# Two diffusion layers on one core: the high halves of the mixers' weight blocks move from ScalarE to GpSimd

## Chip, cores and metric

The kernel runs on one core of a Trainium2 chip, in one launch. The metric is device time in microseconds (us), the median of several runs; lower is better.

## What is computed

The reference is a backbone of two layers over 256 latent tokens and 256 context tokens, 1024 features wide. Each layer is a half-step feed-forward block, a mixer with three groups of channels, and a second half-step feed-forward block. All of it is in 32-bit floats. Cut to what matters here:

```python
for l in range(2):
    x     = x     + 0.5 * mx[2] * swiglu(ada_norm(x, ...),     w_ffn_in[l, 0], w_ffn_out[l, 0])
    h_ctx = h_ctx + 0.5 * mc[2] * swiglu(ada_norm(h_ctx, ...), w_ffn_in[l, 0], w_ffn_out[l, 0])
    # mixer: one projection hx @ w_in, hc @ w_in, split into
    #   q, k, v      -> head norms, rotary, attention
    #   u, g         -> conv of width 4, gates, scans both ways, times gelu(g)
    #   b, c, s      -> b * conv3(c * s)
    # each group RMS-normalised, concatenated, times w_out
    out_x, out_c = mixer(ada_norm(x, ...), ada_norm(h_ctx, ...), p, cos, sin, not last)
    x = x + mx[5] * out_x
    x = x + 0.5 * mx[8] * swiglu(ada_norm(x, ...), w_ffn_in[l, 1], w_ffn_out[l, 1])
    # layer 0 does the same for h_ctx
return rms_norm(x, final_norm_g)
```

## The kernel before

Activations lie with features on the 128 partitions and tokens along the free dimension: columns 0 to 255 are context, 256 to 511 latent. The weights are packed on the host as one list of blocks of 128x1024 floats (`PLAN`), in the order in which the program uses them. TensorE multiplies in the fast rounded format fp32r, so each 32-bit operand is split into a rounded high half and a low half that holds the remainder. `mm3` (lines 326 to 328) makes one product of three matmuls: high by high, high by low, low by high. Names in the profile follow from that: `hh`, `hl` are the halves of the normed input, `hi`, `lo` those of a weight block, `gh`, `gl` those of the feed-forward's inner activation, `mh`, `ml` those of the mixer's merged output.

A weight block goes through three stations. SyncE's queue loads it into one of seven `raw` buffers (L147). Then `split` (lines 131 to 133) makes its halves, in one of five pairs of `hi` and `lo` buffers:

```python
def split(hi, lo, src):
    act(hi, src, AF.Copy)                      # L132, ScalarE
    tt(lo, src, f(hi), OP.subtract)            # L133, VectorE
```

Then TensorE uses the halves. With five pairs, the high half of a block can be written only when TensorE is done with the block five before it. `get` (a step's call for its next block) runs `advance`, which splits two blocks ahead of the one asked for.

Of the 310 blocks of 128x1024 that are split in this way, the two mixers use 24 each: four first blocks of the input projection (`mi`), the k and v columns (`kv`, two blocks), the q columns (`q`, four), six more `mi` blocks for the short convolution (`sc` steps), and eight blocks of the output projection (`mo`). The feed-forward blocks (`wi`, `wo`) use the rest.

A mixer is written as small steps (`kv`, `qp`, `ka`, `qb`, `sm`, `tr`, ...), and the tables `ORDER[0]` and `ORDER[1]` give the sequence of the steps by hand. The framework then makes one queue for each engine out of the program, by what each instruction waits for and by its own estimate of when that is ready; each engine takes its queue strictly in order. So when an instruction goes to another engine, a few of its neighbours change places too. In a mixer, VectorE does the remainder `lo`, the rotary products of q and k (`qo`, `q`), the split of their rows (`kr`, `qr`, by way of L132 and L133 too), the taps of the convolutions (`uc`, `sc`), the scans (`tl`) and the row maxima of the scores (`nb`). ScalarE does the exponentials (`P`), the tanh and the logarithms of the gates (`th`, `a`), copies out of PSUM (`kT`, `qT`, `PT`) and the high halves. TensorE transposes the rows of k and q (L697, L735) before it makes scores (L870). GpSimd does nothing but clear five small tiles at the start.

Of the kernel before, what the change touches and what calls it, by code (L numbers as in the profile page):

```python
# [13 lines left out]
OP = mybir.AluOpType  # L14
# [92 lines left out]
def hybrid_block_kernel(ctx: ExitStack, tc, wpk, xin, pp, cc, cct, qkg, rope, lruw, ident, out):  # L107
    nc = tc.nc
# [9 lines left out]
    stt, tt, ts = vec.scalar_tensor_tensor, vec.tensor_tensor, vec.tensor_scalar  # L118

    def f(ap):  # L120
        return ap.bitcast(F32)
# [5 lines left out]
    def T(dt=F32, name="t"):  # L127
        t = tp.tile([128, 512], dt, tag="t", name=name)
        return t

    def split(hi, lo, src):
        act(hi, src, AF.Copy)  # L132
        tt(lo, src, f(hi), OP.subtract)  # L133
# [9 lines left out]
    def dma_to(i):  # L143
        while nxt_dma[0] <= min(i, len(PLAN) - 1):
            j = nxt_dma[0]
            r = raw4("raw")
            nc.sync.dma_start(r, wpk[j])  # L147
            raws[j] = r
            nxt_dma[0] += 1
# [95 lines left out]
    def mod_unit(l, m, t, raw):  # L245
        for v in range(2):
            junk = tp.tile([128, 1024], BF16, tag="t", name="junk")
            stt(junk, raw, 1.0, CB[v], op0=OP.mult, op1=OP.mult, accum_out=mod_col(l, m, t, v))  # L248
        if t == 7:
            mod_finish(l, m, slice(0, 8))  # L250
# [3 lines left out]
    def mod_products(m, b, i, raw):  # L254


        if m == 1 and i == 0:
            mp[b] = bank()
        c = (1 - m) * 256
        for j in range(4):  # L260
            nc.tensor.matmul(mp[b][32 * j:32 * j + 32, c:c + 256], ccT[:, 4 * i + j, :],
                             raw[:, j * 256:(j + 1) * 256], start=i == 0, stop=i == 1)
        if m == 0 and i == 1:
            row = T(name="modrow")
            act(row, mp[b], AF.Copy)
            pt = bank()
            for t in range(4):
                nc.tensor.transpose(pt[:, t * 128:(t + 1) * 128], row[:, t * 128:(t + 1) * 128], idf)
            sums = const.tile([128, 4, 2], F32, tag="psum4", name="psum4", bufs=2)
            vec.tensor_reduce(sums, pt.rearrange("p (t j c) -> p t c j", t=4, j=4)[:, :, 0:2], axis=AX.X, op=OP.add)  # L270
            for v in (1, 0):
                mod_finish(0, v, slice(2 * b, 2 * b + 2), sums[:, 2 - 2 * v:4 - 2 * v])
# [16 lines left out]
    def advance(i):  # L289

        while nxt[0] <= min(i, len(PLAN) - 1):
            j = nxt[0]
            u = PLAN[j]
            r = raws.pop(j)
            if u[0] == "m":
                mod_unit(u[1], u[2], u[3], r)
            elif u[0] == "p":
                mod_products(*u[2:], r)
            elif WPOS[4] <= j < WPOS[HEAD0]:
                parts = [(T(F32R, "w0h"), T(F32R, "w0l")) for _ in range(2)]  # L300
                for p, (hi, lo) in enumerate(parts):
                    split(hi, lo, r[:, p * 512:(p + 1) * 512])
                ready[j] = [tuple(x[:, i * 128:(i + 1) * 128] for x in p) for p in parts for i in range(4)]
            else:
                hi = wp.tile([128, 1024], F32R, tag="hi", name="hi")
                lo = wp.tile([128, 1024], F32R, tag="lo", name="lo")
                split(hi, lo, r)
                if u[0] in ("kv", "q"):
                    ready[j] = (hi, lo)
                else:  # L310
                    ready[j] = [(hi[:, i * 128:(i + 1) * 128], lo[:, i * 128:(i + 1) * 128]) for i in range(8)]
            nxt[0] += 1
            dma_to(j + RAWB)
# [3 lines left out]
    def get(key, ahead=2):  # L317
        n = nw[0]
        assert PLAN[WPOS[n]] == key, (PLAN[WPOS[n]], key)
        advance(WPOS[min(n + ahead, len(WPOS) - 1)])  # L320
        nw[0] += 1
        return ready.pop(WPOS[n])
# [706 lines left out]
    def first_head(h, units):  # L1029
# [10 lines left out]
        def block(b):  # L1040
            advance(PLAN.index(("p", 0, 0, b, 1)))
            for k in (2 * b, 2 * b + 1):
                h.make(k, FULL)
# [147 lines left out]
```

## Time and profile before

| what | value |
|---|---|
| three runs | 1664.17, 1664.75, 1665.06 us; median 1664.75 |
| the profiled execution | 1665.47 us, of which the profile's span is 1663.7 us |
| TensorE (PE) busy | 1620.4 us, 97% of the span, granted clock 0.994 on average |
| VectorE (DVE) busy | 1124.9 us, 68% |
| ScalarE (ACT) busy | 673.9 us, 41% |
| GpSimd (POOL) busy | 0.5 us, five instructions |

The profile shows one execution. A busy share is an average over stages, so it says little about a stage in which another engine sets the pace. The mixers run from about 390 to 605 us (layer 0) and from about 1315 to 1470 us (layer 1) of the span; the feed-forward blocks and the modulation products fill the rest. A row of the timeline gives start, duration, engine, line and operation, and in brackets how long the engine sat idle before it and what ended that.

### The profile page before, as it was taken

How to read it: one execution, taken by the hardware profiler on the slowest of the kernel's cores; microseconds unless marked ns; L12 is line 12 of the kernel's file. 1: busy time of each engine (PE TensorE's matmuls, PEld its weight loads, DVE VectorE, ACT ScalarE, POOL GpSimd, SP SyncE). 2: the span in 40 equal slices, each digit the busy share in tenths (PEclk: the TensorE clock that was granted, in tenths of full speed). 3: DMA queues.
4: the chain of work that ended last, by engine and by line, in shares of the span. 5: the costliest groups of instructions: out<-in, count | busy, mean ns of one | idle time of the engine just before them, and what ended most of it. 6: DMA issues, size and time to landing. Idle time of an engine off the chain costs nothing.

```text
span 1663.7 us, 21498 instructions
## 1 busy us (share of the span) xinstructions
PE 1620.4 (97%) x8396; PEld 1357.9 (82%) x8396; DVE 1124.9 (68%) x1894; ACT 673.9 (41%) x1073; POOL 0.5 (0%) x5
## 2 busy tenths in 40 slices
PE   7999999999999999999999999999999998999997
PEld 3888888889886898888888898888888887788886
DVE  4667757677697676784667665573555678866666
ACT  4432122323877453322223243222223378655453
POOL 0000000000000000000000000000000000000000
PEclk9999999999999999999999999999999999999999
DMA  8555645553321125564555524453444433245551
GB/s 332 179 184 177 219 136 180 176 176 127 114 78 37 41 72 183 188 207 135 176 176 167 165 95 146 165 177 115 152 141 150 152 102 102 83 146 189 184 185 38
DMA packets 68502, 247.25 MB, mean 149 GB/s; under 512 B 7728, under 2 KB 8240, under 8 KB 68400
## 3 DMA queue, kind: packets, MB, share of 16 engines
q1 hardware_dynamic: 67392, 244.87, 44.2%
q8 instruction: 66, 1.08, 0.3%
q10 hardware_dynamic: 1008, 1.00, 0.2%
q14 instruction: 36, 0.29, 0.1%
HBM read 244.80 MB, written 1.05 MB: 148 GB/s over the span
## 4 chain that ended last, share of the span: by engine, by line
PE 92%; DVE 4%; ACT 3%; DMA 1%; issue 0%; DVEq 0%; ACTq 0%; SPq 0%
PE ps L326 25%; PE ps L327 25%; PE ps L328 25%; PE ps L333 7%; PE ps L334 3%; DVE lo L133 1%; PE ps L902 1%; PE ps L801 1%; PE ps L870 1%; ACT hi L132 1%; PE ps L884 1%; PE ps L386 1%; ACT P L874 1%; PE ps L1021 0%; DVE ht L426 0%
## 5 line engine op out<-in xcount | busy, mean ns | idle before, releaser
L132 ACT ACTIVATE hi<-raw 128x1024 fp32r<-128x1024 f32 x310 | 327.7, 1060 | 789.3 <-PE ps L327 576.4
L133 DVE TENSOR_TENSOR lo<-raw,hi 128x1024 fp32r<-128x1024 f32 x310 | 378.6, 1223 | 196.4 <-ACT hi L132 194.8
L326 PE MATMUL ps<-hh,hi 128*128 128x512 f32 (+1 forms) x1344 | 487.1, 367 | 8.6 <-ACT hh L427 8.0
L328 PE MATMUL ps<-hh,lo 128*128 128x512 f32 (+1 forms) x1344 | 489.6, 365 | 0.8 <-DVE lo L133 0.7
L327 PE MATMUL ps<-hl,hi 128*128 128x512 f32 (+1 forms) x1312 | 480.8, 368 | 3.7 <-DVE hl L430 3.6
L248 DVE SCALAR_TENSOR_TENSOR junk<-raw,cb 128x1024 bf16<-128x1024 f32 x256 | 302.0, 1219 | 13.2 <-DMA raw<-in_wpk_dram 13.2
L326 PEld LDWEIGHTS ps<-hh,hi 128*128 128x128 f32 x1344 | 252.3, 190 | 51.6 <-ACT hh L427 9.7
L328 PEld LDWEIGHTS ps<-hh,lo 128*128 128x128 f32 x1344 | 255.3, 190 | 42.5 <-DVE lo L133 2.3
L327 PEld LDWEIGHTS ps<-hl,hi 128*128 128x128 f32 x1312 | 248.0, 189 | 45.7 <-DVE hl L430 5.3
L326 PE MATMUL ps<-gh,hi 128*128 128x512 f32 (+1 forms) x594 | 217.6, 366 | 0.0
L327 PE MATMUL ps<-gl,hi 128*128 128x512 f32 (+1 forms) x594 | 217.1, 365 | 0.0
L328 PE MATMUL ps<-gh,lo 128*128 128x512 f32 (+1 forms) x594 | 217.1, 365 | 0.0
L524 DVE TENSOR_TENSOR gf<-gf,ps 128x512 f32<-128x512 f32 (+1 forms) x68 | 46.2, 679 | 175.7 <-PE ps L328 174.5
L327 PEld LDWEIGHTS ps<-gl,hi 128*128 128x128 f32 x594 | 112.0, 189 | 18.2
L326 PEld LDWEIGHTS ps<-gh,hi 128*128 128x128 f32 x594 | 112.1, 189 | 18.2
L328 PEld LDWEIGHTS ps<-gh,lo 128*128 128x128 f32 x594 | 112.0, 189 | 18.0
L444 DVE SCALAR_TENSOR_TENSOR xT<-ps,modT,xT 128x256 f32<-128x256 f32 x176 | 79.9, 479 | 65.8 <-PE ps L328 55.5
L333 PE MATMUL ps<-hh,hi 128*128 128x512 f32 x320 | 113.2, 399 | 0.0
L334 PE MATMUL ps<-hh,lo 128*128 128x256 f32 x320 | 89.9, 281 | 0.0
L333 PEld LDWEIGHTS ps<-hh,hi 128*128 128x128 f32 x320 | 60.1, 188 | 14.9
L333 PE MATMUL ps<-gh,hi 128*128 128x512 f32 x176 | 62.2, 398 | 0.1
L334 PEld LDWEIGHTS ps<-hh,lo 128*128 128x128 f32 x320 | 60.5, 189 | 0.0
(203 smaller groups left out, 1601.2 us busy)
## 6 DMA issues: line engine op xcount, KB each, us to landing
raw<-in_wpk_dram SPq DMA_DIRECT2D x456, 512.0 KB, 3.3
xT<-in_xin_dram SPq DMA_DIRECT2D x4, 512.0 KB, 5.4
cb<-in_cc_dram SPq DMA_DIRECT2D x4, 512.0 KB, 3.7
lw<-in_lruw_dram SPq DMA_DIRECT2D x2, 512.0 KB, 4.1
out_dram<-y SPq DMA_DIRECT2D x2, 256.0 KB, 2.7
out_dram<-y ACTq DMA_DIRECT2D x2, 256.0 KB, 2.8
pps<-in_pp_dram ACTq DMA_DIRECT2D x1, 138.0 KB, 6.5
qkb<-in_qkg_dram ACTq DMA_DIRECT2D x1, 128.0 KB, 3.2
```

Of the source, the lines that this page charges most:

```text
L132: act(hi, src, AF.Copy)
L133: tt(lo, src, f(hi), OP.subtract)
L248: stt(junk, raw, 1.0, CB[v], op0=OP.mult, op1=OP.mult, accum_out=mod_col(l, m, t, v))
L326: nc.tensor.matmul(ps, wh, xh, start=first, stop=False)
L327: nc.tensor.matmul(ps, wh, xl, start=False, stop=False)
L328: nc.tensor.matmul(ps, wl, xh, start=False, stop=last)
L333: nc.tensor.matmul(ps, wh, xx, start=first, stop=False)
L334: nc.tensor.matmul(ps[:, 0:256], wl, xx[:, 0:256], start=False, stop=last)
L386: nc.tensor.matmul(st[:, a:b], ones[n], x[:, a:b], start=i == 0, stop=i == len(parts) - 1)
L444: stt(xT[:, k, a:b], ps[:, a - left:b - left], mod_col(l, m, k, v), xT[:, k, a:b], op0=OP.mult, op1=OP.add)
L524: tt(gf[:, a:b], gf[:, a:b], pu[:, a:b], OP.mult)
L801: nc.tensor.matmul(ps, lw[:, c * 128:(c + 1) * 128], uc, start=True, stop=True)
```

## The change

In `advance`, blocks of the kinds `mi`, `kv`, `q` and `mo` get their high half from GpSimd instead of ScalarE; VectorE makes the low half as before. Feed-forward blocks are left with `split`.

```diff
                 hi = wp.tile([128, 1024], F32R, tag="hi", name="hi")
                 lo = wp.tile([128, 1024], F32R, tag="lo", name="lo")
-                split(hi, lo, r)
+                if u[0] in ("mi", "kv", "q", "mo"):
+
+                    nc.gpsimd.tensor_copy(hi, r)
+                    tt(lo, r, f(hi), OP.subtract)
+                else:
+                    split(hi, lo, r)
```

Lines behind the edit move down by five, and the remainder of a mixer block is L310 instead of L133. GpSimd's queue is, behind the clearing of `ccT` at the start, the 48 copies (`CAST hi<-raw 128x1024`, L309) with nothing between them. The queues of the other engines change in some places, by the framework's own choice; three of them are shown, all on VectorE.

The first place is in the mixer of layer 1, where the gates end: `ge` is the gelu, `a` the gate product, `th` and `tl` its input and its scan. Before:

```order
L792 SCALAR_TENSOR_TENSOR ge<-ge,g 128x256
L813 SCALAR_TENSOR_TENSOR a_11104<-a_11104,tl 128x512
L133 TENSOR_TENSOR lo<-raw,hi 128x1024
L828 TENSOR_TENSOR th<-th,a_11104 128x512
L832 SCALAR_TENSOR_TENSOR tl<-th 128x256
L834 SCALAR_TENSOR_TENSOR tl<-th,tl 128x256
```

Now:

```order
L797 SCALAR_TENSOR_TENSOR ge<-ge,g 128x256
L310 TENSOR_TENSOR lo<-raw,hi 128x1024
L818 SCALAR_TENSOR_TENSOR a_11104<-a_11104,tl 128x512
L833 TENSOR_TENSOR th<-th,a_11104 128x512
L837 SCALAR_TENSOR_TENSOR tl<-th 128x256
L839 SCALAR_TENSOR_TENSOR tl<-th,tl 128x256
```

A `lo` (that of the last block of q columns) has moved ahead of the gate product.

The second place is some rows later in the same mixer, where the first rows of q get their rotary products (`q`, `qo`, with the small head norm `hr`) and are split into `qr`. Before:

```order
L666 TENSOR_TENSOR q_11372<-ps,rope_615 128x8x32
L650 TENSOR_SCALAR hr<-hr 128x16
L667 TENSOR_TENSOR qo<-qo,q_11372 128x512
L651 SCALAR_TENSOR_TENSOR hr<-hr 128x16
L668 TENSOR_TENSOR qo<-qo,hr 128x512
L133 TENSOR_TENSOR lo<-raw,hi 128x1024
L133 TENSOR_TENSOR qr<-qo,qr 128x4x64 x2
```

Now:

```order
L671 TENSOR_TENSOR q_11372<-ps,rope_615 128x8x32
L655 TENSOR_SCALAR hr<-hr 128x16
L672 TENSOR_TENSOR qo<-qo,q_11372 128x512
L656 SCALAR_TENSOR_TENSOR hr<-hr 128x16
L310 TENSOR_TENSOR lo<-raw,hi 128x1024
L673 TENSOR_TENSOR qo<-qo,hr 128x512
L133 TENSOR_TENSOR qr<-qo,qr 128x4x64 x2
```

The `lo` has moved ahead of the last rotary product; it stands ahead of `qr` in both.

The third place is in the mixer of layer 0, from the first to the second rows of q; `uc` is the recurrent group's output. Before:

```order
L133 TENSOR_TENSOR qr<-qo,qr 128x4x64 x2
L832 SCALAR_TENSOR_TENSOR tl<-th 128x256
L828 TENSOR_TENSOR th<-th,a_3503 128x512
L659 TENSOR_TENSOR qo<-ps,qkb 128x512
L834 SCALAR_TENSOR_TENSOR tl<-th,tl 128x256
L668 TENSOR_TENSOR qo<-qo,hr 128x512
L133 TENSOR_TENSOR lo<-raw,hi 128x1024
L133 TENSOR_TENSOR qr<-qo,qr 128x4x64 x2
L842 TENSOR_TENSOR uc<-tl 128x512
L832 SCALAR_TENSOR_TENSOR tl<-th 128x256
L843 SCALAR_TENSOR_TENSOR uc<-uc,ge 128x512
```

Now:

```order
L839 SCALAR_TENSOR_TENSOR tl<-th,tl 128x256
L673 TENSOR_TENSOR qo<-qo,hr 128x512
L847 TENSOR_TENSOR uc<-tl 128x512
L133 TENSOR_TENSOR qr<-qo,qr 128x4x64 x2
L310 TENSOR_TENSOR lo<-raw,hi 128x1024
L664 TENSOR_TENSOR qo<-ps,qkb 128x512
L848 SCALAR_TENSOR_TENSOR uc<-uc,ge 128x512
L673 TENSOR_TENSOR qo<-qo,hr 128x512
L833 TENSOR_TENSOR th<-th,a_3503 128x512
L133 TENSOR_TENSOR qr<-qo,qr 128x4x64 x2
```

Two operations on `uc` of 128x512 have moved ahead of the second `qr`; the `lo` that stood ahead of it still does.

## Rows read from the trace of the kernel before

**Rows 1.** The page, part 1: busy time, share, instructions; part 4: the chain.
```profile
PE 1620.4 (97%) x8396; PEld 1357.9 (82%) x8396; DVE 1124.9 (68%) x1894; ACT 673.9 (41%) x1073; POOL 0.5 (0%) x5
PE 92%; DVE 4%; ACT 3%; DMA 1%; issue 0%; DVEq 0%; ACTq 0%; SPq 0%
```

**Rows 2.** Busy time by stage: first mixer, feed-forward blocks, second mixer; then PE, PEld, DVE, ACT.
```profile
390.00:605.00 215.00, 209.49 (x1280) 176.48 (x1280) 161.35 (x310) 141.28 (x281) 0.00 (x0) 1.00 0.21 70
605.00:1315.00 710.00, 709.48 (x3373) 598.14 (x3373) 450.73 (x680) 208.14 (x266) 0.00 (x0) 1.00 0.48 157
1315.00:1470.00 155.00, 139.80 (x933) 119.89 (x933) 124.59 (x237) 108.12 (x208) 0.00 (x0) 0.97 0.29 96
```

**Rows 3.** The page, part 5: the two halves of a weight block.
```profile
L132 ACT ACTIVATE hi<-raw 128x1024 fp32r<-128x1024 f32 x310 | 327.7, 1060 | 789.3 <-PE ps L327 576.4
L133 DVE TENSOR_TENSOR lo<-raw,hi 128x1024 fp32r<-128x1024 f32 x310 | 378.6, 1223 | 196.4 <-ACT hi L132 194.8
```

**Rows 4.** Groups of GpSimd's instructions, whole span.
```profile
L169 POOL MEMSET ccT<- 128x256 f32 x1 | 0.3, 312 | 0.3 <-POOLq L1179 0.3
L1179 POOL MEMSET const-float32-0.0<- 128x1 f32 x1 | 0.1, 99 | 0.2 <-issue 0.2
```

**Rows 5.** Groups of VectorE's instructions by form, 1363.6 to 1384.1 us.
```profile
L133 DVE TENSOR_TENSOR lo<-raw,hi 128x1024 fp32r<-128x1024 f32 x7 | 8.5, 1219 | 0.7 <-ACT hi L132 0.5
L644 DVE TENSOR_REDUCE hr<-sq 128x8 f32<-128x512 f32 x3 | 1.9, 675 | 0.0
...
L666 DVE TENSOR_TENSOR q<-ps,rope 128x256 f32<-128x256 f32 x2 | 0.8, 418 | 0.0
```

**Rows 6.** Timeline of TensorE, second mixer: two waits for VectorE, one for ScalarE.
```profile
1377.66 1.22 PE L697 MATMUL ps<-idr,kr 128*128 128x128 f32 x12 [0.91 <-DVE kr L133]
1384.62 0.68 PE L735 MATMUL ps<-idr,qr 128*128 128x128 f32 x3 [2.51 <-DVE qr L133]
1414.23 1.09 PE L884 MATMUL ps<-idf,P 128*128 128x128 f32 x8 [1.89 <-ACT PT L889]
```

**Rows 7.** Busy time in one stretch of 5 us behind the second wait; 0.66 is the clock.
```profile
1385.00:1390.00 5.00, 5.00 (x19) 3.57 (x20) 3.89 (x9) 2.27 (x4) 0.00 (x0) 0.66 0.35 108
```

**Rows 8.** Timeline of ScalarE, second mixer: the last high half before `qr`.
```profile
1381.73 1.06 ACT L132 ACTIVATE hi<-raw 128x1024 fp32r<-128x1024 f32 x1 [1.23 <-PE ps L327]
```

**Rows 9.** Timeline of VectorE, second mixer: the gap, and the path to `qr`.
```profile
1362.39 0.69 DVE L813 SCALAR_TENSOR_TENSOR a<-a,tl 128x512 f32<-128x512 f32 x1 [2.23 <-ACT a L812]
1363.61 1.22 DVE L133 TENSOR_TENSOR lo<-raw,hi 128x1024 fp32r<-128x1024 f32 x1 [0.53 <-ACT hi L132]
...
1382.92 1.22 DVE L133 TENSOR_TENSOR lo<-raw,hi 128x1024 fp32r<-128x1024 f32 x1
1384.06 0.75 DVE L133 TENSOR_TENSOR qr<-qo,qr 128x256 fp32r<-128x256 f32 x2
```

**Rows 10.** The chain in order of time, second mixer: ScalarE's part of it.
```profile
1394.49 0.95 ACT hi L132
...
1404.47 0.95 ACT hi L132
```

**Rows 11.** Timeline of ScalarE, first mixer: the first and last of four high halves.
```profile
452.46 1.06 ACT L132 ACTIVATE hi<-raw 128x1024 fp32r<-128x1024 f32 x1
...
470.46 1.07 ACT L132 ACTIVATE hi<-raw 128x1024 fp32r<-128x1024 f32 x1
```

**Rows 12.** Timeline, first mixer: VectorE's wait and its `qr`; TensorE's transpose of `qr`.
```profile
464.19 1.23 DVE L133 TENSOR_TENSOR lo<-raw,hi 128x1024 fp32r<-128x1024 f32 x1 [0.73 <-ACT hi L132]
...
473.72 0.75 DVE L133 TENSOR_TENSOR qr<-qo,qr 128x256 fp32r<-128x256 f32 x2
474.39 0.68 DVE L842 TENSOR_TENSOR uc<-tl 128x512 f32<-128x512 f32 x1
...
474.62 0.85 PE L735 MATMUL ps<-idr,qr 128*128 128x128 f32 x8
```

**Rows 13.** Timeline of VectorE, start of the second mixer.
```profile
1323.96 1.23 DVE L133 TENSOR_TENSOR lo<-raw,hi 128x1024 fp32r<-128x1024 f32 x1 [0.34 <-ACT hi L132]
```

## The prediction

> **What bounds the kernel now.** I read the page's busy shares and its chain first [rows 1]. TensorE is busy for 97% of the span and has 92% of the chain, so there is little to win anywhere: only time in which TensorE stands still can be saved. The table by stage says where it stands still [rows 2]. Over the 710 us of feed-forward blocks between the mixers it idles 0.5 us, in the first mixer 215.00 - 209.49 = 5.5 us, in the second 155.00 - 139.80 = 15.2 us. Both mixers together can give back 20.7 us at the very most, 1.2%. In the second mixer VectorE is busy for 124.59 of 155 us and ScalarE for 108.12; neither is full, so which one TensorE waits for has to be read place by place, from the timeline. In the second mixer I use three waits of TensorE [rows 6]: 0.91 and 2.51 us for rows of k and q that VectorE splits, 1.89 us for a copy that ScalarE makes. Behind the longest one the granted clock is 0.66 on average over 5 us [rows 7], so part of that time ran at 1.2 GHz instead of 2.4.
>
> **What the change takes away and adds.** It takes 48 high halves of 1060 ns each from ScalarE [rows 3], 50.9 us, and gives 48 copies to GpSimd, which had nothing to do. VectorE keeps its 48 low halves of 1223 ns. The loads, the buffers and TensorE's matmuls are the same. SyncE's queue issues the same loads; a `raw` buffer comes free when the low half is done, so a load moves only as far as that does. GpSimd's queue holds nothing but the copies, so a copy that waits for its buffer blocks no other work there; the low half behind it on VectorE does block VectorE's queue, as it did before.
>
> *When a copy can run.* It needs the `hi` buffer of the block five before. On ScalarE several high halves waited for just that: the one at 1381.73 us had sat 1.23 us for TensorE [rows 8]. A free engine doesn't get such a buffer earlier.
>
> *How long a copy takes.* GpSimd shows two lengths, 312 ns for clearing 256 columns and 99 ns for one [rows 4], so 213 / 255 = 0.84 ns a column on top of 0.1 us: 0.95 us for 1024. That only writes; if reading took turns with writing it would be 1.9 us. ScalarE's copy of the same shape takes 1.06 [rows 3]. I take 0.95, the engine's own rate.
>
> By the Trainium skill (GPSIMD Engine Reference, section "Performance versus the Vector engine") the best case of a loop is about 1.8 cycles an element at 1.2 GHz, which makes an estimate of 1.54 us for 1024 columns. No run here shows it yet; by it the sum below would come out 5 to 6 us higher.
>
> *What a copy costs VectorE.* This decides the sign, and no row has the two engines side by side. The lower end is 0: they don't disturb each other. The upper end is 1.9 us, VectorE held for the longer of the two copy lengths. I take the middle, one copy of 0.95 us, cut by the share of VectorE's time that goes to reductions and to operands in PSUM: of 20.5 us in the dense stretch `hr` alone has 1.9 and `q` 0.8 [rows 5]; with the smaller groups of the kind I set it at a fifth. That leaves 0.95 x 0.8 = 0.76 us a copy wherever VectorE has no gap, and nothing where it has one.
>
> By the Trainium skill (SBUF — State Buffer, section "Who interferes with whom") a VectorE instruction with both inputs in SBUF and a GpSimd instruction that reads SBUF exclude each other, and the later one waits for the whole of the other. That speaks against this change: every `lo` has two such inputs. By it the sum stays where I put it; without it, it falls to the first rival's.
>
> *Second mixer, the way to `qr`.* From 1363.6 to 1384.1 us VectorE has next to no gap, 0.7 us ahead of its seven `lo` and none elsewhere [rows 5], and TensorE waits for its result [rows 6]. Seven low halves lie in it [rows 5]; the first moves out of it (below), which leaves six copies, the last at about 1381.73 [rows 8]. That one comes when VectorE has only its `lo` to do next, so it costs nothing extra; five cost 5 x 0.76 = 3.8 us. Against that, the `lo` at 1363.61 has moved ahead of the gate product (first place shown of the order), into the gap of 2.23 us [rows 9]: that frees 1.14 us, the distance from a `lo` to the next start [rows 9], and the 0.53 us that it waited, 1.7 us. Net +2.1 us at `qr`. TensorE's earlier wait of 0.91 us doesn't add: it lies on the same engine's way and is absorbed in the later one. The wait grows from 2.51 to 4.6 us, and the low clock behind it, which took 0.34 x 5 = 1.7 us in [rows 7], may last longer; +0.5. Place: **+2.6 us**.
>
> *Second mixer, ScalarE's chain.* From 1391 to 1414 us the chain runs on ScalarE, and two high halves lie in it, 0.95 us each [rows 10]: 1.9 us go. I count 1.3, since the row maxima `nb` that feed the exponentials come from VectorE at nearly the same pace and a part comes back as a wait for them. **-1.3 us**.
>
> *First mixer.* TensorE has slack nearly everywhere, but not at 474.62 us: the transpose starts 0.23 us after VectorE went on from the second `qr` [rows 12]. Ahead of it there are four copies, where ScalarE made them from 452.46 to 470.46 us [rows 11], 4 x 0.76 = 3.0; two operations on `uc` have moved ahead (third place of the order), 0.6 us each start to start, 1.2; the wait of 0.73 us for ScalarE's high half falls away [rows 12], and I count 1.0 for other short gaps, since ScalarE has four high halves less there. 3.0 + 1.2 - 1.7 - 0.2 = **+2.3 us**.
>
> *Starts of the mixers.* VectorE normalises there with no gap. A wait of 0.34 us for a high half goes [rows 13], one copy of 0.76 comes in, in a chain that ends in waits of TensorE: **+0.5 us** for the two. All other copies (tail of each mixer, 420 to 450 us) fall where TensorE has work in hand and VectorE has gaps; I count them at nothing. If that cover is thinner than I think, each costs at most its 0.76.
>
> *Sum.* 2.6 - 1.3 + 2.3 + 0.5 = +4.1 us on the profiled execution's 1665.47, so 1669.6. That execution is 0.72 above the median of the three runs, 1664.75; in medians I predict **1668.9 us**, +0.25%. A measurement of this kernel can tell about 0.2%, 3.3 us, from no change.
>
> **The rivals.**
>
> *The engines don't disturb each other.* Price per copy 0. Then `lo` stands first in line at 1381 us and waits for GpSimd, which waits for TensorE: without the wait of 0.91 the buffer is free at 1380.8; copy 0.95, `lo` 1.14, `qo` 0.6, half of `qr` 0.4 and two handovers of 0.1 end at 1384.1, where it was 1384.6: -0.4 or so, not the 1.7 that VectorE frees. ScalarE's chain gives 1.6. The first mixer gives 0: 1.2 of `uc` against 0.73 and 0.5 of gaps. The start gives 0.3. Sum -2.3: 1662.4 us, which counts as no change; if the shorter wait also spares the low clock, another 1.7 go: 1660.7, faster. For it: VectorE's queue is shorter before `qr`, and ScalarE loses 50.9 us. Against it: it needs two engines to read SBUF side by side at full pace. The sign turns at about 0.4 us a copy: ten copies were charged above, and 1.7 + 1.3 + 0.7 + 0.3 = 4.0 us won stand against them.
>
> *The copy is slow.* At 1.54 to 1.9 us, the upper part of the bounds, a copy costs VectorE 1.2 to 1.5 us. The way to `qr` gives 5 x 1.23 - 1.7 + 1 = +5.5, the first mixer 4 x 1.23 + 1.2 - 1.9 = +4.2, the starts +1, ScalarE's chain -1: +9.7, 1674.5 us. For it: the one row of GpSimd that I have only writes. Against it: nothing in the trace.
>
> *Nothing reaches TensorE.* The high halves that went waited mostly for TensorE (576.4 of 789.3 us of ScalarE's idle time before them, [rows 3]), so ScalarE's relief is idle time only, and the first mixer swallows the rest: gains and losses within 2 us, 1665 us.
>
> **How the numbers follow.** I give the forecast 0.40 (of it 0.31 slower by over 0.2%, 0.09 within), no disturbance 0.33 (0.17 faster, 0.15 within, 0.01 slower), the slow copy 0.14 (all slower), nothing reaching TensorE 0.13 (0.01 faster, 0.11 within, 0.01 slower). Faster 0.18, within 0.2% 0.35, slower 0.47. The range goes from 1660.5, the first rival with the clock regained, to 1676, the slow copy and a little more; about 1 in 6 is left outside. The slower cases alone span 1668 to 1676.
>
> **What would show it.** Right: 48 casts of about 0.95 us on GpSimd; the mean of `lo` in the mixers well above 1223 ns, or casts much longer than 0.95 where VectorE is full; the wait for `qr` in the second mixer longer than 2.51 us and a new wait at the same transpose in the first; ScalarE's chain shorter by one to two us. Wrong: `lo` still at 1.22 us next to a running cast, and the wait for `qr` shorter or the same; that is the first rival. Casts of 1.5 us and more are the second. If TensorE's idle time in both mixers is the same to within 1 us, the third.

## The result, and the profile of the changed kernel

The changed kernel takes **1683.72 us** (median of 3 runs, 1681.58 to 1687.06) against 1664.75: the ratio is 1.0103, with a 95% interval of 1.0086 to 1.0121. It is 19.0 us slower. The forecast was slower, by 4.1 us; the range ended at 1676.0. The profiled execution took 1687.06 us, the longest of the three; its span, 1685.3 us, is 21.6 longer than the span before, 1663.7.

The page's parts 1 and 4, to be read against [rows 1]:

```profile
PE 1630.2 (97%) x8396; PEld 1362.0 (81%) x8396; DVE 1142.0 (68%) x1894; ACT 628.6 (37%) x1025; POOL 62.2 (4%) x53
...
PE 87%; DVE 4%; issue 4%; ACT 3%; DMA 1%; POOL 1%; ACTq 0%; DVEq 0%; SPq 0%; POOLq 0%
```

GpSimd took over what it was given and is busy for 4%, ScalarE lost 45 us. The two halves of the moved blocks, from part 5, to be read against [rows 3]:

```profile
L309 POOL CAST hi<-raw 128x1024 fp32r<-128x1024 f32 x48 | 61.7, 1292 | 1403.1 <-PE ps L332 1337.9
...
L310 DVE TENSOR_TENSOR lo<-raw,hi 128x1024 fp32r<-128x1024 f32 x48 | 62.7, 1318 | 32.6 <-POOL hi L309 32.6
```

A copy took 1.29 us on average, a low half beside them 1.32 instead of 1.22. That is not much: 48 x 0.1 = 5 us of VectorE's time. No engine became the bound; TensorE has less of the chain, 87% instead of 92%. The rows of the two mixers in the table by stage, with the columns of [rows 2] and GpSimd's behind them, show where:

```profile
390.00:605.00 215.00, 204.62 (x1201) 168.94 (x1200) 161.85 (x293) 113.16 (x248) 26.44 (x21) 0.98 0.20 67
...
1315.00:1470.00 155.00, 138.15 (x897) 116.57 (x897) 119.27 (x212) 78.06 (x167) 29.91 (x23) 0.94 0.28 94
```

The windows are cut at fixed times, so a later kernel has less of the second mixer in its window. But the first mixer stands out at once: TensorE idles 10.4 us there where it idled 5.5, and the granted clock fell in both mixers. These rows of TensorE's timeline have the waits that are new or longer by over 0.4 us:

```profile
430.75 7.08 PE L806 MATMUL ps<-uc,lw 128*128 128x512 f32 x12 [3.17 <-issue]
...
481.85 0.89 PE L740 MATMUL ps<-idr,qr 128*128 128x128 f32 x8 [2.43 <-DVE qr L133]
...
1365.06 3.75 PE L806 MATMUL ps<-uc,lw 128*128 128x512 f32 x4 [3.28 <-issue]
...
1396.11 1.22 PE L702 MATMUL ps<-idr,kr 128*128 128x128 f32 x12 [2.34 <-DVE kr L133]
...
1405.68 0.80 PE L740 MATMUL ps<-idr,qr 128*128 128x128 f32 x3 [3.63 <-DVE qr L133]
```

Two stand ahead of the gates' matmuls on `uc`, where the kernel before has no wait recorded; one is new at `qr` of the first mixer; those for `kr` and `qr` of the second mixer have grown from 0.91 and 2.51 us [rows 6]. The profile names no releaser for the first two ("issue"); that they wait for the taps is read from the times in the next section. Together the five make 3.17 + 3.28 + 2.43 + 1.43 + 1.12 = **11.4 us**. Nearly all of the rest is the clock. These are all the stretches of both mixers at a granted clock of 0.5, that is 1.2 GHz, after the change (length, TensorE's busy time with its matmuls, clock, DMA share, GB/s):

```profile
431.96:435.37 3.41, 3.41 (x5) 0.50 0.49 163
483.16:486.57 3.41, 3.41 (x10) 0.50 0.29 89
527.53:530.94 3.41, 3.41 (x6) 0.50 0.00 0
1363.80:1370.62 6.82, 5.56 (x9) 0.50 0.35 109
1397.93:1401.34 3.41, 3.41 (x18) 0.50 0.71 217
1404.76:1411.58 6.82, 5.90 (x16) 0.50 0.24 79
1486.68:1490.09 3.41, 3.41 (x18) 0.50 0.00 0
sum 30.69, PE 28.51; mean PE 4.07
```

and before:

```profile
1386.29:1389.70 3.41, 3.41 (x13) 0.50 0.19 73
1461.38:1468.20 6.82, 5.12 (x24) 0.50 0.11 41
sum 10.23, PE 8.53; mean PE 4.26
```

Work at 1.2 GHz takes twice its time at 2.4, so half of the busy time in such a stretch is lost. The twelve matmuls of the gates show it: they took 7.08 us with 3.41 us of such a stretch in them, and 5.39 without one (experiment 5), which is 1.69 less. So the clock took 28.51 / 2 - 8.53 / 2 = **10.0 us** more than before. Five of the seven stretches begin within 2 us of the end of one of the five waits above; they hold 21.69 us of work, against 3.41 in the stretch behind the wait for `qr` in the kernel before: (21.69 - 3.41) / 2 = 9.1 of the 10.0 us. Waits and clock make 11.4 + 10.0 = 21.4 of the 21.6 us. So the loss of this execution has two halves of nearly one size, and the second follows the first: behind a wait of 2.3 to 3.6 us another 1.7 to 3 us went.

Two limits belong to that. The stretch at 527.53 us, at the end of the first mixer, follows none of the five waits. Kernels that lost nothing have one in that place too (at 517.42 us in the control of experiment 5), so its 1.7 us isn't shown to be the change's. And a wait doesn't always bring a stretch: the wait of 2.43 us for `qr` in the first mixer had none behind it in experiment 5, and the one of 2.5 us in the second mixer, as long as before, had none in experiment 4. The clock's half is thus a figure of one execution.

### The profile page after: what moved, and what is told of

It is laid out like the page before. It is cut to its first block, busy times and chain, and to the rows that moved or that the text cites. A ratio compares the mean times of both kernels' runs of the same rounds, so it can differ in the third digit from the quotient of the medians.

```text
span 1685.3 us, 21538 instructions
## 1 busy us (share of the span) xinstructions
PE 1630.2 (97%) x8396; PEld 1362.0 (81%) x8396; DVE 1142.0 (68%) x1894; ACT 628.6 (37%) x1025; POOL 62.2 (4%) x53
## 4 chain that ended last, share of the span: by engine, by line
PE 87%; DVE 4%; issue 4%; ACT 3%; DMA 1%; POOL 1%; ACTq 0%; DVEq 0%; SPq 0%; POOLq 0%
PE ps L332 24%; PE ps L331 24%; PE ps L333 24%; PE ps L338 7%; PE ps L339 3%; POOL hi L309 1%; PE ps L907 1%; DVE lo L133 1%; PE ps L875 1%; PE ps L391 1%; PE ps L806 1%; DMA raw<-in_wpk_dram 1%; PE ps L889 1%; DVE lo L310 1%; PE ps L261 0%
## 5 line engine op out<-in xcount | busy, mean ns | idle before, releaser
L132 ACT ACTIVATE hi<-raw 128x1024 fp32r<-128x1024 f32 x262 | 277.5, 1060 | 745.9 <-PE ps L332 524.4
L133 DVE TENSOR_TENSOR lo<-raw,hi 128x1024 fp32r<-128x1024 f32 x262 | 320.4, 1223 | 169.3 <-ACT hi L132 169.0
L333 PEld LDWEIGHTS ps<-hh,lo 128*128 128x128 f32 x1344 | 255.8, 190 | 42.2 <-DVE lo L133 1.5
L309 POOL CAST hi<-raw 128x1024 fp32r<-128x1024 f32 x48 | 61.7, 1292 | 1403.1 <-PE ps L332 1337.9
L310 DVE TENSOR_TENSOR lo<-raw,hi 128x1024 fp32r<-128x1024 f32 x48 | 62.7, 1318 | 32.6 <-POOL hi L309 32.6
```

What stands on the lines that cost most here:

```text
L309: nc.gpsimd.tensor_copy(hi, r)
L310: tt(lo, r, f(hi), OP.subtract)
L333: nc.tensor.matmul(ps, wl, xh, start=False, stop=last)
```

## What happened in the two places

First the gates, in the first mixer. When the buffers of four blocks come free at once, GpSimd makes four copies in a row. The timeline of GpSimd, then of VectorE:

```profile
420.69 5.99 POOL L309 CAST hi<-raw 128x1024 fp32r<-128x1024 f32 x4 [23.64 <-PE ps L332]
```
```profile
421.76 4.01 DVE L310 TENSOR_TENSOR lo<-raw,hi 128x1024 fp32r<-128x1024 f32 x2 [9.09 <-POOL hi L309]
425.69 5.62 DVE L787 SCALAR_TENSOR_TENSOR uc<-up,pps,uc 128x512 f32<-128x512 f32 x6
...
429.91 1.40 DVE L787 SCALAR_TENSOR_TENSOR uc<-up,pps,uc 128x512 f32<-128x512 f32 x2
```

Two low halves took 4.01 us instead of 2.36, the six taps of the convolution 5.62 instead of 4.06 (the same queue without reading, experiment 1). Copies and VectorE's operations took turns. The kernel before has only one low half ahead of the taps here; the changed queue has two, but by experiment 1 that order alone makes no wait. The gates wait for the taps. The last line has the fifth and sixth tap alone; the fifth ended at about 430.65 and TensorE started at 430.75. In the kernel before, the same two taps and the first two gates' matmuls, from VectorE's and TensorE's timelines:

```profile
427.28 1.41 DVE L782 SCALAR_TENSOR_TENSOR uc<-up,pps,uc 128x512 f32<-128x512 f32 x2
```
```profile
428.13 1.10 PE L801 MATMUL ps<-uc,lw 128*128 128x512 f32 x2
```

A tap takes 0.75 us, so the fifth ended at 428.03, and TensorE started 0.10 us later. It was there already: no wait was recorded, but there was no slack either. In the second mixer it is the same: the third tap (the first of two from 1349.78 us) ends at 1350.53, and the gates start at 1350.62. The change also put all six taps in a row there, behind two low halves, so that the gates now follow the fifth; experiment 1 has that order too, and no wait.

Second, the way to `qr`. Three rows of VectorE and one of GpSimd, second mixer after the change:

```profile
1388.47 2.06 DVE L310 TENSOR_TENSOR lo<-raw,hi 128x1024 fp32r<-128x1024 f32 x1
...
1391.76 1.03 DVE L133 TENSOR_TENSOR kr<-qo,kr 128x256 fp32r<-128x256 f32 x2 [0.48 <-ACT kr L132]
...
1402.80 1.23 DVE L310 TENSOR_TENSOR lo<-raw,hi 128x1024 fp32r<-128x1024 f32 x1 [0.94 <-POOL hi L309]
```
```profile
1393.84 4.26 POOL L309 CAST hi<-raw 128x1024 fp32r<-128x1024 f32 x1 [1.66 <-PE ps L333]
```

A low half beside a copy took 2.06 instead of 1.22, the pair of `kr` 1.03 instead of 0.75. Then VectorE was in front, in a run of operations with two inputs in SBUF, and a copy took 4.26 us: it ended at 1398.10, 1.0 us after VectorE's next reduction started at 1397.11. Last, a `lo` stands ahead of `qo` and `qr` and waits 0.94 us for its copy, which waits for TensorE's buffer. From the first `th` behind the gate product to `qr`, VectorE took 23.26 us (1381.85 to 1405.11) where it took 19.17 (1364.89 to 1384.06), 4.1 more. Of these, 2.3 are four operations beside copies, all of them before 1393 us (beside the two above, a scan and a rotary product, 0.6 and 0.55 us longer). The other 1.9 are waits: this 0.94, and 0.48 each for ScalarE's halves of `kr` and `qr`, which a low half in VectorE's queue had covered before.

## The experiments

Most kernels choose the blocks by their rank in a mixer (24 blocks each, in the order of use). Only that condition is shown for them; the rank is one dictionary, the rest of the change stays.

**1. The write without the read.** GpSimd clears the `hi` buffer to a constant, so the products are not those of the reference. The order on every engine is that of the changed kernel.

```diff
-                    nc.gpsimd.tensor_copy(hi, r)
+                    nc.gpsimd.memset(f(hi), 0.015625)
```

> The 48 copies on GpSimd become 48 fills of the same tiles with 1/64: they write and read nothing. High halves are therefore a constant and the low half is the rest, so only the rounding differs. The queues of TensorE, VectorE and ScalarE are the same, row by row, as those of the change. Theory A (GpSimd's reading and VectorE's two-source operations exclude each other): the loss goes, 1661 to 1665 us, low halves back at 1.22 us. Theory B (the loss comes from the queues' new order and from waiting for another engine): stays at 1680 us or more. Theory C (writing excludes as well): in between or as the change, low halves longer than 1.3 us.

Measured: 1668.22 us against 1667.02 of the kernel before on that chip, ratio 1.0005 [0.9995, 1.0016]. That is above theory A's range, and so is the kernel before in these runs. The order, the handovers and ScalarE's relief are all in this kernel, and the loss is gone; so the loss comes of the copies' reading. VectorE's timeline in the first burst, at its undisturbed pace:

```profile
421.53 2.36 DVE L309 TENSOR_TENSOR lo<-raw,hi 128x1024 fp32r<-128x1024 f32 x2 [9.32 <-POOL hi L308]
423.81 4.06 DVE L786 SCALAR_TENSOR_TENSOR uc<-up,pps,uc 128x512 f32<-128x512 f32 x6
```

TensorE has no wait ahead of the gates in either mixer, and 0.40 us at `qr` of the first. One wait does not go with the reading: `qr` of the second mixer, TensorE's timeline, and VectorE's rows on the way to it.

```profile
1387.36 0.80 PE L739 MATMUL ps<-idr,qr 128*128 128x128 f32 x3 [4.09 <-DVE qr L133]
```
```profile
1369.73 0.98 DVE L649 TENSOR_SCALAR hr<-hr 128x8 f32<-128x8 f32 x1
...
1378.67 1.22 DVE L309 TENSOR_TENSOR lo<-raw,hi 128x1024 fp32r<-128x1024 f32 x1
...
1381.00 1.22 DVE L309 TENSOR_TENSOR lo<-raw,hi 128x1024 fp32r<-128x1024 f32 x1
...
1384.48 1.22 DVE L309 TENSOR_TENSOR lo<-raw,hi 128x1024 fp32r<-128x1024 f32 x1
...
1386.78 0.76 DVE L133 TENSOR_TENSOR qr<-qo,qr 128x256 fp32r<-128x256 f32 x2 [0.48 <-ACT qr L132]
```

It is 1.6 us longer than before, and that is the order's: three low halves stand between `kr` and `qr` where two stood, 1.14 us, and VectorE waits 0.48 us for ScalarE's half of `qr`, which the last low half covered before [rows 9]. None of the three waits for a buffer. The first row shows something else: this small operation with one input took 0.17 us before, and here, beside a fill, 0.98. A second one took 0.72 instead of 0.16. So the writes did not leave every operation of VectorE as it was; the low halves kept their 1.22 us.

**2. The two engines side by side.** Behind the kernel before: phases of eight copies on GpSimd and eight operations on VectorE that don't depend on each other.

```diff
+    phase("copy", None)
+    phase(None, "tt")
+    phase("copy", "tt")
+    phase("copy", "red")
+    phase("copy", "ps")
+    phase("set", "tt")
```

> The kernel before with a tail: phases of eight GpSimd operations of 128x1024 beside eight of VectorE. Copies alone; two-source subtraction alone; copies beside subtractions; copies beside reductions of one SBUF tensor; copies beside copies out of PSUM; fills beside subtractions. Theory A: beside subtractions the two engines alternate, a pair takes 1.04 + 1.22 = about 2.2 us, and copies beside reductions or PSUM sources, and fills beside subtractions, keep 1.04 us and 1.22 us. If nothing excludes: 1.22 us a pair throughout. If any read of SBUF by both excludes: reductions lengthen as well.

One run, 1718.68 us with the added phases. The first two phases fell beside the end of the kernel itself. VectorE's queue has most of its copies out of PSUM between the reductions, so one phase of GpSimd's copies stands beside both. The timelines of GpSimd (copies beside low halves; beside reductions and copies out of PSUM; then clearing) and of VectorE (low halves beside copies, one copy out of PSUM and one reduction, low halves beside clearing):

```profile
1666.67 14.86 POOL L1113 CAST bhi<-bsrc 128x1024 fp32r<-128x1024 f32 x8 [0.57 <-DVE bsrc L1126]
...
1683.36 7.92 POOL L1113 CAST bhi<-bsrc 128x1024 fp32r<-128x1024 f32 x8 [0.54 <-DVE bsrc L1126]
...
1706.55 6.28 POOL L1115 MEMSET bhi<- 128x1024 f32 x7
```
```profile
1667.01 15.59 DVE L1118 TENSOR_TENSOR blo<-bsrc,bother 128x1024 fp32r<-128x1024 f32 x8
...
1684.86 0.68 DVE L1122 COPY bt<-ps 128x512 f32<-128x512 f32 x1
1685.46 1.20 DVE L1120 TENSOR_REDUCE bsink<-bsrc 128x8 f32<-128x1024 f32 x1
...
1706.65 9.17 DVE L1118 TENSOR_TENSOR blo<-bsrc,bother 128x1024 fp32r<-128x1024 f32 x8 [0.83 <-POOL bsrc L1125]
```

Beside reductions of one input and copies out of PSUM, eight copies take 7.9 us, 0.99 each, and VectorE loses nothing: a reduction takes 1.20 us there, and 1.20 behind the copies' end, at 1692.36. Beside low halves both stretch: 15.59 / 8 = 1.95 us for a low half, against 9.17 / 8 = 1.15 beside clearing. A copy costs VectorE 0.80 us where it has no gap; 0.76 was on the record.

**3. Which blocks.** Five kernels split the 48 copies by their place. First all but the burst (blocks 6 to 10 of each mixer, ten copies), then the burst alone:

```diff
-                if u[0] in ("mi", "kv", "q", "mo"):
+                if RANK.get(j, 5) not in range(5, 10):
```

> The sixth to tenth block of each mixer (the burst of copies when the first four blocks' buffers come free) goes back to ScalarE, 38 copies stay on GpSimd. Theory A with the burst as the main place (it holds up the convolution that the gates' matmuls wait for): 19 us less some 11, 1671 to 1675 us. Rival (every copy costs alike): 19 x 38/48 = 15 us, 1680 us.

```diff
-                if u[0] in ("mi", "kv", "q", "mo"):
+                if RANK.get(j, 0) in range(5, 10):
```

> Only the sixth to tenth block of each mixer goes to GpSimd, 10 copies. Theory A with the burst as the main place: 1673 to 1677 us. Rival (every copy costs alike): 19 x 10/48 = 4 us, 1669 us.

Measured: 1676.82 us, 1.0059 [1.0043, 1.0075], without the burst, between theory and rival; 1677.46 us, 1.0061 [1.0045, 1.0077], with the burst alone, half a microsecond above the theory. Against the 1667.02 us of the kernel before in these runs that is +9.8 and +10.4, the whole loss and a little more. TensorE's timeline of the second kernel has the gates' waits and hardly more (one wait for `re` of 2.31 us instead of 1.55); the wait for `qr` is that of [rows 6]:

```profile
430.08 7.08 PE L809 MATMUL ps<-uc,lw 128*128 128x512 f32 x12 [3.35 <-issue]
...
1358.04 2.60 PE L809 MATMUL ps<-uc,lw 128*128 128x512 f32 x4 [3.44 <-issue]
...
1393.60 0.80 PE L743 MATMUL ps<-idr,qr 128*128 128x128 f32 x3 [2.51 <-DVE qr L137]
```

Then the first five and last six blocks of each mixer (22 copies), and the eight between the burst and those (16 copies):

```diff
-                if u[0] in ("mi", "kv", "q", "mo"):
+                if RANK.get(j, 5) not in range(5, 18):
```

> GpSimd rounds 22 of the 48 blocks: the first five of each mixer and the last six. The ten of the two bursts and the sixteen on the way to q's and k's rows stay on ScalarE. Theory (the place decides: a copy costs only where a result of VectorE is waited for by TensorE soon after): no loss, 1665 to 1669 us, within 0.2% of the kernel before, although the copies last 1.04 to 1.3 us and lengthen VectorE's operations beside them; this also tests my words that the copies of the tails count at nothing. Rival (each copy costs its share wherever it stands, 19 us over 48 copies, 0.4 us each): 22 x 0.4 = 8.7 us, 1674 us.

```diff
-                if u[0] in ("mi", "kv", "q", "mo"):
+                if RANK.get(j, 0) in range(10, 18):
```

> GpSimd rounds only the 16 blocks on the way to the rows of k and q, eight in each mixer (the 11th to the 18th block). Theory (the part of the loss that stays when the burst is given back sits here, and the starts and tails cost nothing): 1673 to 1676 us, +7 to +10. My words on the record put +2.6 - 1.3 + 2.3 = +3.6 us on these copies: 1668 to 1670 us. If it comes out at 1667 or less, the copies cost only together with those of the burst.

Measured: 1668.21 us, 1.0006 [0.9995, 1.0016], for the starts and tails; 1677.46 us, 1.0063 [1.004, 1.0085], for the way to `qr`, a little above the theory's 1676. 22 copies can't be told from none and 16 cost 10.4 us: the place decides. TensorE's waits for `kr` and `qr` with the 16 alone, first the first mixer:

```profile
477.49 1.26 PE L743 MATMUL ps<-idr,qr 128*128 128x128 f32 x8 [3.38 <-DVE qr L137]
...
1386.02 1.22 PE L705 MATMUL ps<-idr,kr 128*128 128x128 f32 x12 [2.34 <-DVE kr L137]
...
1395.59 0.81 PE L743 MATMUL ps<-idr,qr 128*128 128x128 f32 x3 [3.64 <-DVE qr L137]
```

They make 3.38 + 1.43 + 1.13 = 5.9 us. The five stretches at half clock, in the same view as above,

```profile
sum 23.87, PE 21.20; mean PE 4.24
```

hold 21.20 us of TensorE's work against 8.53 before, which is 6.3 us lost (1.7 of it in a stretch at 523.90 us, a place where kernels without a loss have one too). The sum, 12.3, answers to the span's growth to 1675.7, 12.0 us. Last, the 17th and 18th block of each mixer; the 17th had the longest copy in both, 2.55 and 4.26 us:

```diff
-                if u[0] in ("mi", "kv", "q", "mo"):
+                if RANK.get(j, 0) in (16, 17):
```

> GpSimd rounds only the 17th and 18th block of each mixer, four copies in all: those beside VectorE's work on the rows of q, of which one took 4.26 us in the second mixer and one 2.55 us in the first. Theory (the long copies next to the wait do the most harm): the wait for q's rows grows by about 1 us in the second mixer and appears in the first; +3 to +5, 1669 to 1671 us. Rival (the loss is the sum of small delays of the eight copies, and the last two are no worse): at most +2, 1665 to 1668 us.

Measured: 1667.82 us, 1.0006 [0.9996, 1.0017]: in time, the rival. The wait for `qr` grew to 3.4 us in the second mixer, but no wait came up in the first. None of the four copies lasted longer than 2.18 us here, so what a copy of 4.26 us does by itself stays untested; the run shows that these four don't make the loss of the 16 by themselves.

**4. ScalarE's chain.** Only the two high halves of [rows 10] go to GpSimd.

```diff
-                if u[0] in ("mi", "kv", "q", "mo"):
+                if u[0] == "mo" and u[1:] in ((1, 0, 2), (1, 0, 3)):
```

> Only the two output blocks of the second mixer whose high halves lay in ScalarE's chain (1394 and 1404 us) go to GpSimd. If ScalarE sets the pace there: 1.3 to 1.9 us less than before, 1663 us. If the row maxima on VectorE pace it, or the copies hold up VectorE: within 0.7 us of before.

Measured: 1669.13 us, 1.0009 [1.0, 1.0018]. No gain; the 1663 us of a ScalarE that sets the pace are out. ScalarE's timeline in the place, and TensorE's wait behind it:

```profile
1409.96 1.08 ACT L136 ACTIVATE hi<-raw 128x1024 fp32r<-128x1024 f32 x1
```
```profile
1416.11 1.09 PE L892 MATMUL ps<-idf,P 128*128 128x128 f32 x8 [2.50 <-ACT PT L897]
```

The next block's high half, which ran at 1420.72 before, moved up into the room that the two had left, and the wait was 2.50 us instead of 1.89 [rows 6].

**5. The taps first.** All 48 copies on GpSimd, but on VectorE the two low halves ahead of the taps go behind them; then the same order with ScalarE making the copies, as a control; then the first with the 16 blocks on the way to `qr` given back to ScalarE.

```diff
+            if j in held:
+                break
...
+            if ct == 1:
+                five = next(i for i, n in RANK.items() if n == 5 and PLAN[i][1] == l)
+                held.discard(five)
+                with tc.issue_after(last_tap.ins):
+                    advance(five + 1)
```

> The change as it is, all 48 copies on GpSimd, but in both mixers the two low halves that stand ahead of the six taps of the convolution on VectorE are placed behind them. The four copies of the burst still run at the same time. Theory (the gates' wait is made by the two low halves, 2.0 us each, that wait for slow copies ahead of the taps): the taps end 3 to 4 us earlier, the waits of 3.17 and 3.28 us ahead of the gates' matmuls go with the low clock behind them, and of the 19 us some 10 are regained: about 1673 to 1675 us; the loss on the way to q's and k's rows stays. Rival (VectorE's lost time is only moved: the low halves come later, and TensorE waits for them or for k's rows instead): 1680 us or more.

> The kernel before with the same order of VectorE, the low halves behind the taps, and ScalarE making every high half: the control for the run with the taps first. TensorE has no wait ahead of the gates in the kernel before, so both theories expect no change, 1663 to 1668 us. Were it faster by over 0.2%, part of what the other run regains would be the order's own and not the copies'.

> The change with the taps first, and with the 16 blocks on the way to q's and k's rows given back to ScalarE: GpSimd keeps 32 copies, those of the bursts among them. Theory (the loss has two places, the taps and the way to q's rows, and nothing else): 1665 to 1669 us, the kernel before. Rival (with the taps first, the burst's time on VectorE is only paid a little later, at the rows of k): 1671 to 1674 us, with a wait for them that is 2 us longer than before.

Measured: 1679.59 us, 1.0076 [1.005, 1.0102], with the taps first; 1666.81 us, 1.0001 [0.9988, 1.0013], for the control; 1670.92 us, 1.0015 [1.0003, 1.0027], with the 16 given back. The first lies between theory and rival, and so does the third, just under its rival's 1671. TensorE's timeline with the taps first (the profiled execution is the fastest, 1677.34 us):

```profile
427.81 5.39 PE L817 MATMUL ps<-uc,lw 128*128 128x512 f32 x12 [0.28 <-issue]
...
1355.91 1.95 PE L817 MATMUL ps<-uc,lw 128*128 128x512 f32 x4 [0.45 <-issue]
...
1387.51 1.54 PE L708 MATMUL ps<-idr,kr 128*128 128x128 f32 x12 [4.87 <-DVE kr L137]
```

Both gates' waits are gone, as the theory has it. In the first mixer that is a gain. In the second the wait for `kr` grew from 2.34 to 4.87 us: there the rival is right, VectorE's time is only paid later. The third kernel, without the copies on the way, is nearly at the kernel before, and not below it. Its waits for `kr` and `qr` are 1.02 and 2.52 us, so the late payment needs the copies on the way as well. But its profiled execution took 1666.38 us, the fastest of ten; where the slower ones lost their time no trace shows. No run found a version that beats the kernel before.

## Why the prediction was right in its direction and wrong in its size

*The mechanism* was right: the engines exclude each other where VectorE has two inputs in SBUF and GpSimd reads. The rule of the Trainium skill (SBUF — State Buffer, section "Who interferes with whom") says just that, and that a GpSimd instruction which only writes doesn't contend with two-input ones; experiments 1 and 2 agree for the low halves, 1.95 us beside copies and 1.15 beside clearing. The small one-input operations that lasted longer beside a fill in experiment 1 (0.98 us instead of 0.17) were in no term. Without the rule the forecast would have gone over to the first rival.

*The price of a copy*, 0.76 us, was right: 0.80. *The length of a copy*, 0.95 us, was 0.99 undisturbed and 1.29 on average (61.7 us for 48). The estimate of 1.54 us by the Trainium skill (GPSIMD Engine Reference, section "Performance versus the Vector engine") is not borne out: the copies were not slow by themselves, and the second rival falls.

*The waits at `qr`* came out near the forecast, in part by luck. "+2.1 us at `qr`" for the second mixer: the waits for `kr` and `qr` grew by 2.55 together. But the parts are others. "five cost 5 x 0.76 = 3.8 us" was 2.3, in four operations; the 1.7 us that the moved `lo` was to free shrank to 0.4, since VectorE then waited for ScalarE's `a`; and 1.9 us of waits came up that the sum did not have: the `lo` that waits for its copy ahead of `qr`, which was the first rival's thought, and ScalarE's halves of `kr` and `qr`. "TensorE's earlier wait of 0.91 us doesn't add" was wrong: it grew to 2.34. "+2.3 us" for the first mixer: 2.43, but with TensorE already held up at the gates; without that it is 3.38 (experiment 3).

*The step that failed first* is "All other copies (tail of each mixer, 420 to 450 us) fall where TensorE has work in hand and VectorE has gaps; I count them at nothing". For the starts and tails it holds (experiment 3, 1.0006). For the bursts it is wrong: ten copies cost 10.4 us. VectorE does have gaps there, 9.1 us idle ahead of the burst (the row of its two low halves), but the copies don't fall into the gap: they come all at once when it ends. TensorE frees the buffers, and the end of the first copy is what lets VectorE go on. And TensorE's work in hand ended 0.1 us behind the fifth tap. I had the two rows and didn't set one against the other; the second mixer's burst, at 1355 us, I did not cost at all.

*The step that failed second* is the low clock, "+0.5". It was taken for one wait that gets longer. In the profiled execution each of the five waits has its own stretch at 1.2 GHz, and all stretches together took 10.0 us more than before. With the 6.3 us that the clock took in experiment 3, the two `qr` terms come to 2.1 + 2.3 + 6.3 = 10.7, near the 10.4 us of the 16 copies.

*ScalarE's chain*, "-1.3 us", gave next to nothing: in the changed kernel TensorE's two waits in it, for `P` and `PT`, went from 1.00 and 1.89 us to 1.04 and 1.70, and experiment 4 shows no gain. The most that any trace has is 0.7 us, in experiment 1 (0.46 and 1.70).

So in the sum: 2.6 + 2.3 was about 10, the bursts' 0 was about 10, -1.3 was -0.2, and the 0.5 for the starts fits TensorE's waits for `hh` there (0.87 us in both mixers, 0.64 and 0.51 before), though no time tells it from 0.

## What to carry to other kernels

Work that moves to GpSimd and reads SBUF is not free where VectorE works on two SBUF inputs: cost it at nearly a copy's length (0.80 us for one of 0.99). Beside reductions and reads of PSUM it was free (experiment 2); no run here placed the copies there. "No wait recorded" is not slack: compare the end of the producer with the start of the consumer, and a difference of 0.1 us means that every delay counts. And a new wait of TensorE is to be costed with the stretch at half clock that may follow it, here nearly as much again as the wait.

## What the runs showed of the hardware that was not expected

- Under load GpSimd and VectorE took turns, one instruction each (two low halves in 4.01 us beside four copies in 5.99); but a copy that meets a run of two-input operations of VectorE already under way can be held back through it: 4.26 us instead of 0.99.
- Small one-input operations of VectorE lasted longer beside a fill, which reads nothing: 0.98 and 0.72 us instead of 0.17 and 0.16 (experiment 1). Beside a copy one lasted 1.01 us instead of 0.17, at 497.07 us in the changed kernel.
- The kernel before took 1663.79 to 1670.6 us over 23 later runs, a far wider spread than the 0.9 us of its first three. The mean granted clock goes with it, 0.995 in the fastest and 0.990 in the slowest, so part of what the clock takes comes without any change. The fastest run of the changed kernel, 1681.58 us, is still 11.0 us above the slowest of these. The profiles of experiments 3 and 4 have half-clock stretches in differing places (the two-copies kernel at 1417 and 1428 us, the kernel before at neither); why one run gets them and another not stays open.
